# Four transposes between the products of the tile before, and an add ahead of a copy, in a matmul with bias and residual

## The chip, the cores and the metric

The kernel runs on one core of one Trainium2 chip. The metric is the device time of one execution in microseconds (us); it is given as the median of several runs. A profile is one more execution, recorded instruction by instruction; its span runs from the first to the last recorded instruction and is a little shorter than the device time.

The engines are named as in the profile: PE is TensorE's matmul, PEld its weight load, DVE is VectorE, ACT is ScalarE, POOL is GpSimd, and SP is the engine that issues all the DMAs here.

## What is computed

```python
batch, m, k, n = 16, 512, 1024, 768      # all float32
def reference(x, weight, bias, residual):
    return (np.matmul(x, weight) + bias + residual).astype(np.float32)
```

So 8192 rows of 1024 values are multiplied by one 1024 x 768 matrix, and a bias row and a residual of the output's shape are added.

## The kernel before

The 8192 rows are 64 tiles of 128 rows. Four groups of 16 tiles (S = 0 to 3) share the layout of the loads: row p*16 + j of a group is partition p of tile j, so that one DMA can bring several tiles.

A tile passes through these steps:

1. Its x arrives in a slot of `X` (16 slots). `cast` (lines 234 to 244, through `copy`, line 226) turns the 128 x 1024 float32 values into bfloat16 in `XB` (4 buffers); in the loop ScalarE does this, two tiles ahead.
2. `transp` (lines 246 to 253) takes two neighbouring bfloat16 values as one 32-bit word. TensorE transposes the 128 x 512 words in four steps of 128 x 128 into a PSUM buffer `PT` (2 buffers; line 250). The words themselves are the weights of such a step, and a float32 identity streams through. Then VectorE copies the whole buffer, 128 x 1024 as bfloat16, to `XT` (4 buffers; line 226).
3. `mm_all` (273 to 276) runs eight products, for q in 0..3 and e in 0..1. Each (`mm`, 265 to 271) loads 128 x 128 weights from `XT` (line 268) and streams 768 columns of the weight matrix as two matmuls of 512 and 256 columns (line 257), all into one PSUM accumulator `PO` of 128 x 768 float32. There are three of these (`HEAD = 3`).
4. `finish` (300 to 308) is VectorE's final add of a tile. For tiles below 14 it adds the bias to `PO` and puts the sum into a spare row; GpSimd adds the residual later. From tile 14 on, GpSimd has already added bias and residual in place (`pool_adds`, 286 to 298), and VectorE adds `PO` to that; it therefore waits for GpSimd.
5. The finished rows are stored from `R` by SP, in groups of up to 16 tiles.

The first tiles run in an order written out by hand (`HEAD_ORDER`), because there weights are still arriving; products of tiles 0 to 2 are interleaved, and the transposes of tiles 0 to 3 are done there. Tile 0's `finish` stands in that list too. The loop then takes tiles 3 to 62, and in each turn t the instructions are recorded in this order:

```python
    for t in range(HEAD, n_t):
        cast(t + 2)
        pool_adds(t + 1)
        transp(t + 1)
        if t < n_t - 1:
            mm_all(t, range(n_q))
        finish(t - 1)
        pool_adds(t + 1)
```

The last tile's products run column block by column block behind the loop (512 columns, then 256), so that the first block can be added and stored under the second.

`Program` keeps this recorded order on each engine: every engine runs its own instructions strictly in it. Between engines it derives waits from what an instruction reads and writes: a product's first weight load waits for VectorE's copy into `XT`, a first transpose for ScalarE's cast into `XB`, a copy for the fourth transpose, a first product into `PO` for the `finish` of the tile three before.

SP has one list of DMAs (`ORDER`), which goes on only when the first entry's needs have been recorded. On the chip SP also waits, at each DMA, for the work whose buffer it overwrites or stores.

Of the kernel before, what the change touches and what calls it, by code (L numbers as in the profile page):

```python
# [8 lines left out]
FP32 = mybir.dt.float32  # L9
BF16 = mybir.dt.bfloat16  # L10
P = 128
# [4 lines left out]
HEAD = 3  # L16
XT_N = 4
XB_N = 4
WARM = 12
EARLY_END = 14  # L20
TMP_ROW = 16
W_ROW = 14
# [95 lines left out]
def kernel(  # L118
# [14 lines left out]
    n_q = K // (2 * P)  # L133
    n_t = M // P
    chunks = [(0, 512), (512, N - 512)]
# [9 lines left out]
    def fixed(pool, name, n, shape, dt):  # L145
        return [pool.tile(shape, dt, name=f"{name}", tag=f"{name}{i}", bufs=1) for i in range(n)]
# [3 lines left out]
    XB = fixed(sb, "xb", XB_N, [P, K], BF16)  # L150
    XT = fixed(sb, "xt", XT_N, [P, n_q, P, 2], BF16)
    PO = fixed(ps, "psum_o", HEAD, [P, N], FP32)
    PT = fixed(ps, "pt", 2, [P, n_q, P], FP32)
# [8 lines left out]
    op = prog.add  # L162

    def rows(a, b, cs=range(len(chunks))):
        return [("R", r % RR, c) for r in range(a, b) for c in cs]
# [8 lines left out]
    def pump():  # L174
        while queue:
# [7 lines left out]
            elif kind == "r":  # L183
# [4 lines left out]
                if S < RR // J:  # L188
                    need += [("add", t) for t in range(EARLY_END) if TMP_ROW + t in at]
            else:  # L190
# [30 lines left out]
    def mark(*what):  # L221
        done.add(what)
        pump()

    def copy(eng, dst, src, rd, wr):
        op(eng, lambda e: (e.copy if eng == "act" else e.tensor_copy)(out=dst, in_=src), rd, wr)  # L226

    def plus(eng, dst, a, b, rd, wr):
        op(eng, lambda e: e.tensor_add(out=dst, in0=a, in1=b), rd, wr)  # L229
# [4 lines left out]
    def cast(t, how="s"):  # L234
        if t < n_t:
            assert ("x", t) in done, t
            src, dst, h = X[:, t % XR, :], XB[t % XB_N], K // 2
            rd, wr = [("X", t % XR)], [("XB", t % XB_N, i) for i in range(2)]
            if how == "sv":
                copy("act", dst[:, 0:h], src[:, 0:h], rd, wr[:1])  # L240
                copy("dve", dst[:, h:K], src[:, h:K], rd, wr[1:])
            else:
                copy("act" if how == "s" else "dve", dst, src, rd, wr)
            mark("cast", t)

    def transp(t):
        if t < n_t:
            words, pt = XB[t % XB_N].bitcast(FP32), PT[t % 2]
            for q in range(n_q):
                op("pe", lambda e, q=q: e.transpose(out=pt[:, q, :], in_=words[:, ts(q, P)], identity=ident),  # L250
                   [("XB", t % XB_N, 2 * q // n_q), "ident"], [("PT", t % 2)])
            copy("dve", XT[t % XT_N].rearrange("p q m e -> p (q m e)"),
                 pt.rearrange("p q m -> p (q m)").bitcast(BF16), [("PT", t % 2)], [("XT", t % XT_N)])

    def times(po, lhsT, rhs, first, final, rd, wr):
        def emit(e):
            return e.add_instruction(mybir.InstMatmult(  # L257
                name=nc.get_next_instruction_name(),
                ins=[e.lower_ap(rhs), e.lower_ap(lhsT, for_matmul_weights=True)], outs=[e.lower_ap(po)],
                start_tensor_calc=first, stop_tensor_calc=final,  # L260
                tile_size=(P, P), tile_position=(0, 0), ldweights=False,
            ))
        op("pe", emit, rd, wr)

    def mm(t, q, e, parts, po, wr):

        lhsT, rd = XT[t % XT_N][:, q, :, e], [("XT", t % XT_N)]
        op("pe", lambda g: g.ldweights(lhsT), rd)  # L268
        for n0, nl, to in parts:
            times(po[:, to:to + nl], lhsT, w_sb[:, q, e, n0:n0 + nl], q == 0 and e == 0, q == n_q - 1 and e == 1,  # L270
                  [*rd, ("w", q, e)], [wr])

    def mm_all(t, qs):
        for q in qs:
            for e in range(2):
                mm(t, q, e, [(n0, nl, n0) for n0, nl in chunks], PO[t % HEAD], ("PO", t % HEAD))

    def row(t, n0=0, nl=N):
        return R[:, t % RR, n0:n0 + nl]

    def tmp(t):
        return R[:, TMP_ROW + t, :]
# [3 lines left out]
    def pool_adds(upto):  # L286
        for t in [t for t in adds if t <= upto]:
            if ("r", t) not in done or (t < EARLY_END and ("fin", t) not in done):
                return
            adds.remove(t)  # L290
            r, rk = row(t), rows(t, t + 1)
            if t < EARLY_END:
                plus("pool", r, r, tmp(t), rk + rows(TMP_ROW + t, TMP_ROW + t + 1), rk)
                mark("add", t)
                mark("out", t)
            else:
                plus("pool", r, r, bias_sb, rk + ["bias"], rk)
                mark("add", t)

    def finish(t):  # L300
        p, pk = PO[t % HEAD], ("PO", t % HEAD)
        if t < EARLY_END:
            plus("dve", tmp(t), p, bias_sb, [pk, "bias"], rows(TMP_ROW + t, TMP_ROW + t + 1))
            mark("fin", t)
        else:
            assert ("add", t) in done, t
            plus("dve", row(t), p, row(t), [pk] + rows(t, t + 1), rows(t, t + 1))
            mark("out", t)

    def dummies(n, i):  # L310
        for _ in range(n):
            op("pe", lambda e: e.matmul(PO[i][:, 0:512], lhsT=warm[:, 0:P], rhs=warm, start=True, stop=True),  # L312
               ["warm"], [("PO", i)])
# [7 lines left out]
        out=ident, in_=ident, compare_op=mybir.AluOpType.not_equal, fill=1.0, base=0,  # L321
        pattern=[[-1, P]], channel_multiplier=1,
    ), ["ident"], ["ident"])
    dummies(WARM, 0)

    pump()
    for kind, *a in HEAD_ORDER:
        if kind == "bias":
            op("dve", lambda e: e.stream_shuffle(out=bias_sb, in_=bias_row, mask=[0] * QUAD), ["bias_row"], ["bias"])  # L329
        elif kind == "cast":  # L330
            cast(*a)
        elif kind == "fin":
            finish(a[0])
        elif kind == "warm":
            dummies(a[0], HEAD - 1)
        elif kind == "tr":
            transp(a[0])
        elif kind == "wc":
            q, e, eng = a
            r = W_ROW + 2 * q + e  # L340
            copy({"v": "dve", "s": "act", "g": "pool"}[eng], w_sb[:, q, e, :], w_st[:, 2 * q + e, :], rows(r, r + 1), [("w", q, e)])
            if (q, e) == (n_q - 1, 1):
                mark("wcast", q)
        else:
            mm_all(a[0], [a[1]])
    pump()
    for t in range(HEAD - 1):
        if ("fin", t) not in done:
            finish(t)
        pool_adds(t)  # L350

    for t in range(HEAD, n_t):
        cast(t + 2)
        pool_adds(t + 1)
        transp(t + 1)
        if t < n_t - 1:
            mm_all(t, range(n_q))
        finish(t - 1)
        pool_adds(t + 1)
    t = n_t - 1  # L360
    for i, (n0, nl) in enumerate(LAST):
# [46 lines left out]
```

## Time and profile before

| what | value |
|---|---|
| device time, median of 3 runs | 210.47 us (210.31 to 210.57) |
| span of the profiled execution | 208.5 us |
| PE busy | 201.6 us |
| VectorE, ScalarE, GpSimd busy | 105.3, 66.1, 115.2 us |
| mean granted TensorE clock | 0.996 |
| bytes moved | 87.20 MB, mean 418 GB/s |
| one product matmul of 512 columns, of 256 columns (mean length) | 379 ns, 273 ns |
| one transpose (mean length) | 274 ns |
| a copy `PT` to `XT` on VectorE | 691 ns |
| a final add on VectorE | 949 ns |
| a residual sum on GpSimd | 1817 ns |

The device time is taken outside the profile, and the span lies about 2 us below it. Matmuls are pipelined: the length of one includes its way through the array, and the next starts earlier, so a stream's pace is read from the distance of starts and not from the lengths. A line in the timeline merges neighbouring instructions of one kind; its second number is the time from the first start to the last end. In square brackets is the engine's idle time just before, and what ended it.

### The profile page before, as it was taken

What the parts mean: (1) busy time and instruction counts of PE and PEld (TensorE: products, weight loads), DVE (VectorE), ACT (ScalarE), POOL (GpSimd) and SP (SyncE); (2) the same over time, 40 slices, a digit from 0 to 9 for tenths busy, and PEclk for the clock granted to TensorE, in tenths of its full rate; (3) what the DMA queues carried; (4) which work ended last, traced back from release to release, by engine and by line L of the source; (5) the groups of instructions that cost most, each with busy time, mean ns of one, the idle gap of its engine ahead of it and who ended that gap; (6) DMA issues with size and microseconds to landing.
All of it is one profiled execution on the core that took longest, in us unless ns stands there. A gap on an engine that the chain in (4) does not pass through costs nothing.

```text
span 208.5 us, 2492 instructions
## 1 busy us (share of the span) xinstructions
PE 201.6 (97%) x1298; PEld 80.8 (39%) x794; DVE 105.3 (51%) x141; ACT 66.1 (32%) x69; POOL 115.2 (55%) x71
## 2 busy tenths in 40 slices
PE   7899999999999999999999999999999999999991
PEld 2333434443443444344334434433443443344340
DVE  1457555445545543654554454555445545544542
ACT  2444522402640282420280094230092047430000
POOL 1100029859999904999029801999207960899200
PEclk9999999999999999999999999999999999999998
DMA  5999999899999999999998999999999999999985
GB/s 216 425 425 445 426 423 475 385 427 425 485 409 416 449 395 438 453 396 437 410 493 387 432 445 429 443 443 385 423 450 468 416 398 471 415 443 417 427 351 232
DMA packets 4627, 87.20 MB, mean 418 GB/s; under 512 B 516, under 2 KB 644, under 8 KB 1416
## 3 DMA queue, kind: packets, MB, share of 16 engines
q1 hardware_dynamic: 4616, 87.05, 97.9%
q8 instruction: 8, 0.13, 0.2%
q14 instruction: 3, 0.02, 0.0%
HBM read 61.88 MB, written 25.17 MB: 417 GB/s over the span
## 4 chain that ended last, share of the span: by engine, by line
PE 92%; DMA 4%; DVE 1%; SPq 0%; ACT 0%; issue 0%
PE psum_o L257 79%; PE pt L250 13%; DMA x_tile<-in_x_dram 4%; SPq L168 0%; DVE xt L226 0%; ACT xb L226 0%; DVE ro L229 0%; SPq L403 0%; SPq L371 0%
## 5 line engine op out<-in xcount | busy, mean ns | idle before, releaser
L257 PE MATMUL psum_o<-w_sb,xt 128*128 128x256 bf16 (+1 forms) x1024 | 176.6, 326 | 0.5 <-DVE xt L226 0.5
L229 POOL TENSOR_TENSOR ro<-ro,bias_sb 128x768 f32<-128x768 f32 x50 | 88.8, 1817 | 46.9 <-DMA ro<-in_residual_dram 46.9
L226 ACT CAST xb<-x_tile 128x1024 bf16<-128x1024 f32 (+1 forms) x63 | 61.3, 1023 | 117.1 <-DMA x_tile<-in_x_dram 88.6
L268 PEld LDWEIGHTS <-xt 128*128 128x128 bf16 x520 | 50.9, 98 | 102.9 <-issue 101.0
L226 DVE COPY xt<-pt 128x1024 bf16<-128x1024 bf16 x64 | 44.1, 691 | 83.4 <-PE pt L250 83.4
L229 DVE TENSOR_TENSOR ro<-psum_o,ro 128x768 f32<-128x768 f32 (+2 forms) x51 | 47.6, 934 | 6.5 <-POOL ro L229 4.5
L250 PE MATMUL pt<-ident,xb 128*128 128x128 f32 x256 | 38.3, 274 | 0.6 <-DVE xb L226 0.4
L229 POOL TENSOR_TENSOR ro<-ro 128x768 f32<-128x768 f32 x14 | 24.9, 1818 | 25.0 <-DMA ro<-in_residual_dram 24.9
L250 PEld LDWEIGHTS pt<-ident,xb 128*128 128x128 f32 x256 | 29.7, 141 | 15.6 <-issue 12.3
L229 DVE TENSOR_TENSOR ro<-psum_o,bias_sb 128x768 f32<-128x768 f32 x14 | 13.2, 948 | 0.0
L312 PE MATMUL psum_o<-warm 128*128 128x512 bf16 x18 | 6.3, 506 | 1.4 <-DVE warm_a L232 1.4
L226 DVE CAST xb<-x_tile 128x512 bf16<-128x512 f32 (+1 forms) x4 | 1.9, 492 | 6.2 <-DMA x_tile<-in_x_dram 6.2
L226 ACT CAST w_sb<-ro 128x768 bf16<-128x768 f32 x4 | 3.3, 832 | 3.7 <-DMA ro<-in_weight_dram 3.7
L226 POOL CAST w_sb<-ro 128x768 bf16<-128x768 f32 x1 | 0.8, 822 | 6.0 <-DMA ro<-in_weight_dram 6.0
L312 PEld LDWEIGHTS psum_o<-warm 128*128 128x128 bf16 x18 | 2.1, 124 | 4.5 <-issue 2.7
L226 DVE CAST w_sb<-ro 128x768 bf16<-128x768 f32 x3 | 1.7, 557 | 2.0 <-DMA ro<-in_weight_dram 2.0
L226 ACT ACT_TABLE_LOAD x1 | 1.3, 1283 | 0.9 <-SPq L371 0.9
L329 DVE STREAM_SHUFFLE bias_sb<-bias_row 128x768 f32<-128x768 f32 x1 | 1.0, 1007 | 0.0
L232 DVE MEMSET warm<- 128x256 uint32 x1 | 0.3, 272 | 1.1 <-SPq L371 1.1
L232 DVE MEMSET bias_row<- 128x768 f32 x1 | 0.7, 698 | 0.2 <-issue 0.2
L232 POOL MEMSET ident<- 128x128 f32 x1 | 0.2, 204 | 0.5 <-SPq L371 0.5
L320 POOL TENSOR_SCALAR_AFFINE_SELECT ident<-ident 128x128 f32<-128x128 f32 x1 | 0.3, 292 | 0.2 <-POOL ident L232 0.2
(7 smaller groups left out, 0.7 us busy)
## 6 DMA issues: line engine op xcount, KB each, us to landing
out_dram<-ro SPq DMA_DIRECT2D x3, 6144.0 KB, 34.6
x_tile<-in_x_dram SPq DMA_DIRECT2D x3, 5120.0 KB, 24.5
ro<-in_residual_dram SPq DMA_DIRECT2D x3, 3840.0 KB, 32.4
x_tile<-in_x_dram SPq DMA_DIRECT2D x3, 3072.0 KB, 34.0
ro<-in_residual_dram SPq DMA_DIRECT2D x3, 2304.0 KB, 18.7
x_tile<-in_x_dram SPq DMA_DIRECT2D x4, 1024.0 KB, 10.9
x_tile<-in_x_dram SPq DMA_DIRECT2D x2, 2048.0 KB, 23.4
out_dram<-ro SPq DMA_DIRECT2D x1, 3840.0 KB, 13.3
```

Of the source, the lines that this page charges most:

```text
L226: op(eng, lambda e: (e.copy if eng == "act" else e.tensor_copy)(out=dst, in_=src), rd, wr)
L229: op(eng, lambda e: e.tensor_add(out=dst, in0=a, in1=b), rd, wr)
L232: op(eng, lambda e: e.memset(dst, v), [], [wr])
L250: op("pe", lambda e, q=q: e.transpose(out=pt[:, q, :], in_=words[:, ts(q, P)], identity=ident), [("XB", t % XB_N, 2 * q // n_q), "ident"], ...
L257: return e.add_instruction(mybir.InstMatmult(name=nc.get_next_instruction_name(), ins=[e.lower_ap(rhs), e.lower_ap(lhsT, for_matmul_weight ...
L268: op("pe", lambda g: g.ldweights(lhsT), rd)
L312: op("pe", lambda e: e.matmul(PO[i][:, 0:512], lhsT=warm[:, 0:P], rhs=warm, start=True, stop=True), ["warm"], [("PO", i)])
L320: op("pool", lambda e: e.affine_select(out=ident, in_=ident, compare_op=mybir.AluOpType.not_equal, fill=1.0, base=0, pattern=[[-1, P]], ch ...
L329: op("dve", lambda e: e.stream_shuffle(out=bias_sb, in_=bias_row, mask=[0] * QUAD), ["bias_row"], ["bias"])
```

## The change

In the loop, `transp(t + 1)` no longer stands ahead of the products of tile t. A new function `woven` runs the eight products of tile t and puts the four transposes of tile t + 1 one by one behind the second, third, fourth and fifth of them. The copy of the four transposes is recorded right behind the fourth, and `finish(t - 1)`, which stood behind it on VectorE, now stands ahead of it. In the last turn (t = 63) only `finish(62)` is left. `HEAD_ORDER` still uses `transp`, now made of the same two parts.

```diff
@@ -17,6 +17,7 @@
 XT_N = 4
 XB_N = 4
 WARM = 12
+WEAVE = 1
 EARLY_END = 14
 TMP_ROW = 16
 W_ROW = 14
@@ -243,14 +244,20 @@
                 copy("act" if how == "s" else "dve", dst, src, rd, wr)
             mark("cast", t)
 
+    def turn(t, q):
+        words, pt = XB[t % XB_N].bitcast(FP32), PT[t % 2]
+        op("pe", lambda e: e.transpose(out=pt[:, q, :], in_=words[:, ts(q, P)], identity=ident),
+           [("XB", t % XB_N, 2 * q // n_q), "ident"], [("PT", t % 2)])
+
+    def turned(t):
+        copy("dve", XT[t % XT_N].rearrange("p q m e -> p (q m e)"),
+             PT[t % 2].rearrange("p q m -> p (q m)").bitcast(BF16), [("PT", t % 2)], [("XT", t % XT_N)])
+
     def transp(t):
         if t < n_t:
-            words, pt = XB[t % XB_N].bitcast(FP32), PT[t % 2]
             for q in range(n_q):
-                op("pe", lambda e, q=q: e.transpose(out=pt[:, q, :], in_=words[:, ts(q, P)], identity=ident),
-                   [("XB", t % XB_N, 2 * q // n_q), "ident"], [("PT", t % 2)])
-            copy("dve", XT[t % XT_N].rearrange("p q m e -> p (q m e)"),
-                 pt.rearrange("p q m -> p (q m)").bitcast(BF16), [("PT", t % 2)], [("XT", t % XT_N)])
+                turn(t, q)
+            turned(t)
 
     def times(po, lhsT, rhs, first, final, rd, wr):
         def emit(e):
@@ -349,13 +356,23 @@
             finish(t)
         pool_adds(t)
 
+    def woven(t):
+
+        for q in range(n_q):
+            for e in range(2):
+                mm(t, q, e, [(n0, nl, n0) for n0, nl in chunks], PO[t % HEAD], ("PO", t % HEAD))
+                i = 2 * q + e - WEAVE
+                if t + 1 < n_t and 0 <= i < n_q:
+                    turn(t + 1, i)
+                    if i == n_q - 1:
+                        turned(t + 1)
+
     for t in range(HEAD, n_t):
         cast(t + 2)
         pool_adds(t + 1)
-        transp(t + 1)
+        finish(t - 1)
         if t < n_t - 1:
-            mm_all(t, range(n_q))
-        finish(t - 1)
+            woven(t)
         pool_adds(t + 1)
     t = n_t - 1
     for i, (n0, nl) in enumerate(LAST):
```

On the engines' queues this moves nothing but the transposes on TensorE and the adds on VectorE. The order on ScalarE, GpSimd and SP is as before. On VectorE an add gets a wait of its own for TensorE's last product; before, the copy ahead of it had already waited for a later TensorE instruction.

## The prediction

> **What bounds the kernel now.** I read the page first, then the waits, then the timeline of four places: one tile in the steady loop, the start of the loop, the first product that waits for a copy, and a tile whose residual comes late.
>
> The page says that TensorE is the bound: busy 97% of the span, at full clock, and the chain that ended last is almost all matmuls. The DMA queue is nearly as full, which matters below.
>
> ```profile
> span 208.5 us, 2492 instructions
> PE 201.6 (97%) x1298; PEld 80.8 (39%) x794; DVE 105.3 (51%) x141; ACT 66.1 (32%) x69; POOL 115.2 (55%) x71
> ...
> q1 hardware_dynamic: 4616, 87.05, 97.9%
> ...
> PE psum_o L257 79%; PE pt L250 13%; DMA x_tile<-in_x_dram 4%; SPq L168 0%; DVE xt L226 0%; ACT xb L226 0%; DVE ro L229 0%; SPq L403 0%; SPq L371 0%
> ```
>
> One tile of the steady loop, in the timeline (start, length, engine, line, what; x is how many were merged):
>
> ```profile
> 101.06 0.47 PEld L250 LDWEIGHTS pt<-ident,xb 128*128 128x128 f32 x4 [0.23 <-issue]
> 101.17 0.60 PE L250 MATMUL pt<-ident,xb 128*128 128x128 f32 x4
> 101.49 0.10 PEld L268 LDWEIGHTS <-xt 128*128 128x128 bf16 x1
> 101.60 2.76 PE L257 MATMUL psum_o<-w_sb,xt 128*128 128x512 bf16 x16
> 101.80 0.69 DVE L226 COPY xt<-pt 128x1024 bf16<-128x1024 bf16 x1 [1.48 <-PE pt L250]
> ...
> 102.41 0.95 DVE L229 TENSOR_TENSOR ro<-psum_o,ro 128x768 f32<-128x768 f32 x1
> ...
> 104.20 0.60 PE L250 MATMUL pt<-ident,xb 128*128 128x128 f32 x4
> ```
>
> The four transposes start at 101.17 and the products at 101.60, so a transpose costs 0.109 us of the stream; the tile period is 104.20 - 101.17 = 3.03 us, which leaves 2.60 for eight products, 0.325 each (216 ns for the 512-wide matmul and 109 for the 256-wide in the trace's nanosecond records). There is no idle time. Every weight load starts as the matmul ahead of it starts, and is hidden under it.
>
> **Part 1, the weave itself.** Per tile the same 8 pairs of matmuls and 4 transposes run. Before, the stream has one step from a product to a transpose (101.06 load, 101.17 transpose), three from transpose to transpose, one from transpose to product (101.49 load, 101.60 product); each is 0.109 us. Woven, it has four steps of the first kind and four of the third, each already seen. Could a transpose get cheaper because its float32 weights now hide under a product? After an idle engine its load is exposed:
>
> ```profile
> 6.51 0.33 PE L250 MATMUL pt<-ident,xb 128*128 128x128 f32 x1 [0.43 <-DVE xb L226]
> ```
>
> This one takes 0.33 instead of 0.27, so the load is worth 0.06, below the 0.109 that it hides under already; and the step from the last transpose to a product, whose bfloat16 load is shorter still, is also 0.109. So it is the transpose's own streaming that takes the time. Cost of part 1: 0. Its lower bound is 0.109 - 0.06 = 0.05 saved on each of 4 x 59 transposes, 11.6 us, if I misread what the 0.109 is; I keep it for a rival.
>
> **Part 2, the hand-off of a tile.** Before, the copy of the next tile's transposes has a whole tile to spare: 101.80 + 0.69 = 102.49, needed at 104.6. Woven, the fourth transpose stands behind the fifth product, so that only three products lie between it and the next tile's first weight load, which waits for the copy. What is available: 0.109 + 3 x 0.325 = 1.084 us from the start of that transpose. What is needed: 0.31 until the copy starts (101.493 to 101.803), 0.69 for the copy, then the signal to TensorE and the exposed part of the weight load. The last two show where a product waited for such a copy in the head:
>
> ```profile
> 11.47 1.29 DVE L226 COPY xt<-pt 128x1024 bf16<-128x1024 bf16 x2 [0.60 <-PE pt L250]
> ...
> 12.21 0.33 PEld L268 LDWEIGHTS <-xt 128*128 128x128 bf16 x2 [0.50 <-DVE xt L226]
> 12.22 0.50 PE L257 MATMUL psum_o<-w_sb,xt 128*128 128x512 bf16 x2 [0.26 <-DVE xt L226]
> ```
>
> The first of the two copies ends at 11.468 + 0.693 = 12.161, the load starts at 12.213 (0.052 later), the product at 12.217 and loses another 0.011 against a normal one: 0.015 behind the load. Sum: 0.310 + 0.692 + 0.052 + 0.015 = 1.069 of 1.084. It fits with 0.015 us to spare, so I take 0; the spread of the 59 steady copies' start is 0.309 to 0.311, which does not use it up. This is the tightest term. From the other side: if a load needed the whole 0.109 that it now has ahead of its matmul, the product would be late by 0.310 + 0.692 + 0.052 + 0.109 - 1.084 = 0.079; with the 0.06 of the transposes' load, by 0.03. I take 0 because the row at 12.21 is the very same load, and because a transposes' load that began 0.017 late (170.92 where the matmul ahead began at 170.90) left its matmul on time at 171.01.
>
> The Trainium skill, "TensorE: Matmul & The Clock Gate", section "LDWEIGHTS (loading the stationary operand)", speaks against this change: it gives a load as the number of columns over 1.2, 107 ns for 128. By it the product would be 0.077 us late in each of 59 tiles, some 4.5 us (an estimate from that page); the row at 12.21 shows 15 ns, and the measurement decides.
>
> **Part 3, the add ahead of the copy.** In the timeline above the add of tile t-1 (line 307, through 229) runs 0.81 us after the first product of tile t, behind the copy. Alone it could start when the last product of t-1 is done, about 0.20 after that point (a 256-wide product's end reaches VectorE 0.31 after its start), and end at 1.15; the fourth transpose starts at 5 x 0.325 + 3 x 0.109 = 1.95 and the copy is due at 1.95 + 0.31 = 2.26. So normally 1.1 us are free and the new place costs nothing. An explicit wait for TensorE is added to it, one queue instruction of about 0.07, inside that. But from tile 14 on the add also waits for GpSimd's sum of residual and bias, and now the copy, and so TensorE, stands behind it. The waits list shows VectorE held that way, and the worst case in the timeline:
>
> ```profile
> DVE ro L229 <- POOL ro L229: 4.5, 5, 1.7
> ```
>
> ```profile
> 80.34 2.76 PE L257 MATMUL psum_o<-w_sb,xt 128*128 128x512 bf16 x16
> ...
> 81.07 5.36 POOL L229 TENSOR_TENSOR ro<-ro,bias_sb 128x768 f32<-128x768 f32 x3 [8.46 <-DMA ro<-in_residual_dram]
> 82.92 0.96 DVE L229 TENSOR_TENSOR ro<-psum_o,ro 128x768 f32<-128x768 f32 x1 [1.68 <-POOL ro L229]
> ...
> 83.38 2.33 PE L257 MATMUL psum_o<-w_sb,xt 128*128 128x512 bf16 x13
> ...
> 83.79 0.68 DVE L226 COPY xt<-pt 128x1024 bf16<-128x1024 bf16 x1
> ```
>
> Here tile 23's products start at 80.34 and the residual of tile 22 has just landed (81.00; GpSimd's sum ends at 82.88). The add starts at 82.92. Before, only the add and a copy not yet needed were late. Woven, the copy for tile 24 comes behind that add: 82.915 + 0.873 (the distance at 83.79) = 83.788, its end 84.470, the product 0.067 later at 84.537. Due was 83.382: TensorE stands still for 1.155 us. The other late tiles, by the same sum: tile 17 (add at 63.80) would be about 0.26 late, 0.1 if GpSimd's chain comes 0.15 earlier thanks to earlier adds; tile 39 (add at 131.395) would have its next product at 133.02, due at 131.97, so 1.05. These are landing times, and they do not add up: once TensorE is 1.155 late, tile 39's residual is no longer late for it. That holds if landings stay where they are, and they should: the queue is full (97.9%), SP's order is unchanged, each long load is issued with over 6 us of earlier transfers still to run. Casts move up to 2 us later where they wait for transposes, and the loads behind them lie under the same backlog. Together: 1.155 (between 0, landings 1.2 us earlier, and 2.5, if every later landing moves with the delay).
>
> **Part 4, the start of the loop.** Tile 4's transposes, first in the loop, now fill a hole:
>
> ```profile
> 18.61 1.82 DVE L229 TENSOR_TENSOR ro<-psum_o,bias_sb 128x768 f32<-128x768 f32 x2
> 19.00 0.66 PE L250 MATMUL pt<-ident,xb 128*128 128x128 f32 x4
> 19.61 0.38 PE L257 MATMUL psum_o<-w_sb,xt 128*128 128x512 bf16 x1
> ```
>
> The first product of tile 3 waits until 19.61 for the first of the two adds (18.61 + 0.95, then 0.05), whatever the transposes do. Woven, these four come after 19.61 and cost 4 x 0.109 = 0.437 us on the stream; nothing gives it back at the other end, since the last tile's transposes stay inside tile 62.
>
> **Part 5, the end.** The last add, the last stores and their landing follow the last product; the DMA engines are 63% busy between 202.0 and 203.5, so the last stores start when issued and shift with TensorE.
>
> **Sum**: 0 + 0 + 1.155 + 0.437 = 1.59 us, on the span of 208.5, 210.1. The median of the runs is 210.47, 1.96 above the span for what lies around it; the same again gives 212.1.
>
> **The rivals.**
> - The hand-off is missed in every tile. For it: 0.015 us of slack on a sum of four terms, one seen in only one row. Against: that row is exact. It decides from 0.015 us more than I count. At 0.03 per tile it costs 59 x 0.03 = 1.8, of which 0.6 come before tile 24 and are part of the 1.155 there: 0.44 + 1.16 + 1.2 = 2.8, 213.2. At 0.079 it has swallowed the late residual: 0.44 + 4.66 = 5.1, 215.6.
> - The residual isn't late. If landings come 1.4% sooner (79.85 instead of 81.00), part 3 is free: 210.47 + 0.44 = 210.9. Against: loads are paced by a full queue. For: this is one execution.
> - Not slower: the transposes themselves get cheaper, a float32 load under a 0.325 us product rather than under the short transpose before it. It decides from 1.59 / 59 = 0.027 us per tile, 7 ns on each transpose. At its full 11.6 us the DMA queue becomes the bound: 0.979 x 208.5 = 204.1 us of transfers, 1.5 before and 1.6 behind them, 207.2 of span, 209.2. Against: the step from transpose to product above.
>
> **How the numbers follow.** Forecast 212.1 with chance 0.63, own range 211.4 to 212.7; hand-off missed 0.20; no late residual 0.11; cheaper transposes 0.06. The range 210.8 to 214.0 takes in the second rival and the lower half of the first, and leaves out about 0.14. A measurement tells 0.2%, 0.42 us, from no change: half of the "no late residual" case falls within it, and a corner of the cheaper transposes: same 0.07, faster 0.05, slower 0.88.
>
> **What would show it.** Right: a tile period of 3.04 as before; one idle stretch of TensorE of some 1.1 us near 83.4 released by the copy, with the add ahead of it released by GpSimd; products of tile 3 at 19.6 with no transposes before them. Wrong: idle time before most tiles' first load, released by the copy (first rival); transposes less than 0.109 apart from the product behind them (third); several late residuals that each stop TensorE.

## The result, and the profile after

| | before | after |
|---|---|---|
| device time, median (range) | 210.52 us (210.31 to 210.59) | 212.10 us (211.81 to 212.27) |
| ratio | | 1.0082, 95% interval 1.0068 to 1.0096 |
| span of the profiled execution | 208.5 us | 210.3 us |

The change makes the kernel 1.58 us slower; 212.1 had been forecast, and slower with 0.88. The page of the kernel after, its span, its engines and the chain that ended last:

```profile
span 210.3 us, 2515 instructions
PE 200.1 (95%) x1273; PEld 80.7 (38%) x794; DVE 110.4 (52%) x141; ACT 66.7 (32%) x69; POOL 115.2 (55%) x71
...
PE 57%; DMA 29%; POOL 10%; issue 1%; DVE 1%; SPq 0%; POOLq 0%
PE psum_o L264 49%; DMA ro<-in_residual_dram 26%; POOL ro L230 9%; PE pt L249 8%; DMA ro<-in_weight_dram 3%; DVE ro L230 0%; POOL w_sb L227 0%; DVE xt L227 0%; SPq L169 0%; SPq L420 0%; POOLq L105 0%; SPq L105 0%; SPq L388 0%
```

(25 product matmuls are missing from this record, 1273 instead of 1298, so PE's busy time reads a little low.) The chain is the news: before, 92% of it was TensorE. Now it goes from TensorE to GpSimd's residual sum and from there to the residual's transfer, which holds 26%.

First the steady tile, in the timeline of the kernel after:

```profile
100.57 0.27 PE L249 MATMUL pt<-ident,xb 128*128 128x128 f32 x1
...
101.00 0.27 PE L249 MATMUL pt<-ident,xb 128*128 128x128 f32 x1
...
101.44 0.27 PE L249 MATMUL pt<-ident,xb 128*128 128x128 f32 x1
...
101.87 0.27 PE L249 MATMUL pt<-ident,xb 128*128 128x128 f32 x1
...
102.18 0.69 DVE L227 COPY xt<-pt 128x1024 bf16<-128x1024 bf16 x1 [1.03 <-PE pt L249]
...
102.93 0.34 PEld L275 LDWEIGHTS <-xt 128*128 128x128 bf16 x2 [0.31 <-DVE xt L227]
103.16 0.96 DVE L230 TENSOR_TENSOR ro<-psum_o,ro 128x768 f32<-128x768 f32 x1 [0.28 <-PE psum_o L264]
...
103.61 0.27 PE L249 MATMUL pt<-ident,xb 128*128 128x128 f32 x1
```

Transposes now stand 0.434 us apart, which is one product (0.325) and one transpose (0.109). The first transposes of two tiles lie 103.61 - 100.57 = 3.04 us apart, the period of before. The hand-off of a tile is the way from its fourth transpose over VectorE's copy to its first product. The load at 102.93 waits for the copy (102.18 + 0.69 = 102.87, and 0.05), and its own idle time of 0.31 shows that; but in the trace's nanosecond records the product behind it starts 1.084 us after the fourth transpose, just when the stream is ready for it. In 58 of the 60 hand-offs that distance is 1.084 or 1.085.

In the other two an add stood ahead of the copy and waited for GpSimd's sum of residual and bias; below they are called the late residuals. Around the larger one, in the same timeline:

```profile
81.03 0.27 PE L249 MATMUL pt<-ident,xb 128*128 128x128 f32 x1
...
81.27 7.12 POOL L230 TENSOR_TENSOR ro<-ro,bias_sb 128x768 f32<-128x768 f32 x4 [8.94 <-DMA ro<-in_residual_dram]
...
82.34 0.27 PE L249 MATMUL pt<-ident,xb 128*128 128x128 f32 x1
82.44 1.14 PE L264 MATMUL psum_o<-w_sb,xt 128*128 128x512 bf16 x5
...
83.11 0.96 DVE L230 TENSOR_TENSOR ro<-psum_o,ro 128x768 f32<-128x768 f32 x1 [2.81 <-POOL ro L230]
83.99 0.68 DVE L227 COPY xt<-pt 128x1024 bf16<-128x1024 bf16 x1
84.73 0.83 PE L264 MATMUL psum_o<-w_sb,xt 128*128 128x512 bf16 x4 [1.14 <-DVE xt L227]
```

The transposes of tile 24 are complete at 82.6, and their copy could start at 82.65. It starts at 83.99, behind an add that waited for GpSimd, which waited for the transfer. The product comes 2.390 us after the fourth transpose instead of 1.084: 1.306 us lost. The same in small in turn 17: 1.256, 0.172 lost. There the add again waited for GpSimd, but no transfer had just landed: GpSimd's sum stood behind its own earlier ones, which ran without a break from 43.94 on.

```profile
61.65 3.58 POOL L230 TENSOR_TENSOR ro<-ro,bias_sb 128x768 f32<-128x768 f32 x2
...
63.57 0.96 DVE L230 TENSOR_TENSOR ro<-psum_o,ro 128x768 f32<-128x768 f32 x1 [1.68 <-POOL ro L230]
64.45 0.68 DVE L227 COPY xt<-pt 128x1024 bf16<-128x1024 bf16 x1
```

And the start of the loop:

```profile
18.46 2.68 DVE L230 TENSOR_TENSOR ro<-psum_o,bias_sb 128x768 f32<-128x768 f32 x3
19.47 0.81 PE L264 MATMUL psum_o<-w_sb,xt 128*128 128x512 bf16 x4 [0.67 <-DVE ro L230]
...
20.12 0.27 PE L249 MATMUL pt<-ident,xb 128*128 128x128 f32 x1
```

TensorE idles before 19.47, where the transposes of tile 4 stood; they follow behind the second product, at 20.12.

From the first product of tile 3 to the last matmul the kernel before takes 203.866 - 19.615 = 184.25 us, the kernel after 205.659 - 19.469 = 186.19. Of these 1.94 us, 1.306 + 0.172 are the late residuals, 0.437 the four transposes, and 0.02 is left.

### The profile page after: what moved, and what is told of

It is laid out like the page before. It is cut to its first block, busy times and chain, and to the rows that moved or that the text cites. A ratio compares the mean times of both kernels' runs of the same rounds, so it can differ in the third digit from the quotient of the medians.

```text
span 210.3 us, 2515 instructions
## 1 busy us (share of the span) xinstructions
PE 200.1 (95%) x1273; PEld 80.7 (38%) x794; DVE 110.4 (52%) x141; ACT 66.7 (32%) x69; POOL 115.2 (55%) x71
## 4 chain that ended last, share of the span: by engine, by line
PE 57%; DMA 29%; POOL 10%; issue 1%; DVE 1%; SPq 0%; POOLq 0%
PE psum_o L264 49%; DMA ro<-in_residual_dram 26%; POOL ro L230 9%; PE pt L249 8%; DMA ro<-in_weight_dram 3%; DVE ro L230 0%; POOL w_sb L227 0%; DVE xt L227 0%; SPq L169 0%; SPq L420 0%; POOLq L105 0%; SPq L105 0%; SPq L388 0%
## 5 line engine op out<-in xcount | busy, mean ns | idle before, releaser
L264 PE MATMUL psum_o<-w_sb,xt 128*128 128x256 bf16 (+1 forms) x999 | 190.9, 324 | 3.6 <-DVE xt L227 1.7
L249 PE MATMUL pt<-ident,xb 128*128 128x128 f32 x256 | 67.7, 273 | 0.8 <-DVE xb L227 0.6
L230 DVE TENSOR_TENSOR ro<-psum_o,ro 128x768 f32<-128x768 f32 (+2 forms) x51 | 48.1, 942 | 21.2 <-PE psum_o L264 14.8
L249 PEld LDWEIGHTS pt<-ident,xb 128*128 128x128 f32 x256 | 35.5, 141 | 56.4 <-issue 48.4
```

Of the source, the lines that this page charges most:

```text
L249: op("pe", lambda e: e.transpose(out=pt[:, q, :], in_=words[:, ts(q, P)], identity=ident), [("XB", t % XB_N, 2 * q // n_q), "ident"], [("P ...
L264: return e.add_instruction(mybir.InstMatmult(name=nc.get_next_instruction_name(), ins=[e.lower_ap(rhs), e.lower_ap(lhsT, for_matmul_weight ...
```

## The experiments

All were timed beside the kernel before on their own chip, which took 210.14 to 210.20 us there; differences are against that.

**The copy ahead of the add again, in every turn.** The transposes stay woven.

```diff
-        finish(t - 1)
         if t < n_t - 1:
             woven(t)
+        finish(t - 1)
```

> The weave is kept, but the final add of tile t-1 is recorded behind the copy again, in every turn. My theory (the weave itself is free; the start of the loop costs 0.44 us; the rest is the copy queued behind adds whose residual is late): no idle time of TensorE near 62 and 82 us, tile period 3.037 us throughout, 0.44 us slower than before: 210.96 us, and 1.1 us faster than the changed kernel. Rival (a little is lost in every one of 60 tiles, 1.58 / 60 = 0.026 us each): order of the add does not matter, 212.1 us.

Measured: 211.46 us, 1.0051 (1.0037 to 1.0065), 1.30 us above before. TensorE stops nowhere between 20 us and its end, as expected, and it ends 0.47 us later than before (last matmul at 204.34 against 203.87). But the expected 210.96 was 0.44 above a kernel before of 210.52, and here it is 1.30: 0.86 more. Neither theory gave this; something behind TensorE had become slower.

**Tile 4's transposes whole, the rest as changed.**

```diff
         pool_adds(t + 1)
+        if t == HEAD:
+            transp(t + 1)
         finish(t - 1)
...
-                if t + 1 < n_t and 0 <= i < n_q:
+                if t > HEAD and t + 1 < n_t and 0 <= i < n_q:
```

> As the changed kernel, but tile 4's four transposes and their copy stand whole ahead of tile 3's products, as before; from tile 4 on all is woven and the add comes first. My theory: the four run in the hole that ends at 19.6 us, 0.44 us are given back, the stop near 82 us stays and can grow, since TensorE comes there no later than in the changed kernel: 211.66 us. Rival (loss in every tile): one woven tile fewer, 212.1 us.

Measured: 211.75 us, 1.0071 (1.0055 to 1.0086), 1.59 above before: by the medians nothing was given back (the two intervals leave room for some 0.4). TensorE has 0.44 us less to do ahead of the late residuals and waits for them all the same: in its profile it loses 0.39 at tile 18, 0.89 at tile 24 and 0.10 at tile 40, 1.37 together, though tile 22's residual landed 0.48 earlier than in the changed kernel (80.713 against 81.196). What fixes the place is that landing: tile 24's first product starts 3.53 us behind it in the changed kernel, 3.52 here, and 3.52 in the kernel below with each transpose one product earlier. I had seen that the stop can grow and not drawn the conclusion: tile 24's product starts when the residual's transfer lets it, whatever stands before it. The two losses are not independent, and mending this one alone brought nothing that the medians show.

**Both.** Copy ahead of the add in every turn, and tile 4's transposes whole.

> Copy ahead of the add in every turn, and tile 4's transposes whole at the start of the loop; tiles 4 to 62 are woven. My theory: both losses gone, the same as before: 210.5 us within 0.15. Rival (0.026 us lost in each of 59 woven tiles): 212.1 us. A rival in which weaving gains but is hidden by the two losses: below 210.3 us.

Measured: 211.05 us, 1.0034 (1.0022 to 1.0046), 0.89 above. No expectation met. Yet the last matmul starts at 203.900, against 203.866 before, and from the first product of tile 3 it is 184.251 us in both: TensorE lost nothing. The 0.9 us lie behind it. The windows of 188 to 192 us show where (PE, PEld, DVE, ACT, POOL busy with counts, granted clock, DMA share, GB/s), first before:

```profile
188.00:192.00 4.00, 4.00 (x28) 1.51 (x15) 1.94 (x3) 0.00 (x0) 4.00 (x3) 1.00 0.99 427
```

```profile
188.41 16.55 SPq L168 DMA_DIRECT2D out_dram<-ro  x5
```

and this experiment, each with SP's timeline:

```profile
188.00:192.00 4.00, 3.95 (x28) 1.62 (x16) 2.03 (x3) 1.04 (x1) 4.00 (x4) 1.00 0.77 332
```

```profile
190.07 15.46 SPq L169 DMA_DIRECT2D out_dram<-ro  x5
```

The DMA engines are 77% busy there instead of 99%. How much that is worth depends on where the window is cut (from 187 to 194 us it is 92% instead of 95%); the landings show it without a window. The store of tiles 48 to 57 is issued at 190.07 and lands at 202.52; before it was issued at 188.41 and landed at 201.69. The last store lands at 208.02 instead of 207.27. The store of tiles 48 to 57 waits for the add of tile 57. With the woven copy ahead of it, an add starts 2.87 us after the next tile's first product; it was 0.81 in the kernel before and mostly 0.20 to 0.27 in the changed one. My reading: the store comes too late to follow the one ahead of it without a break, and the queue has no slack for it later. This was a reading of one profile, so it got its own test:

**Copy first up to turn 49, add first from turn 50 on**, tile 4's transposes whole.

```diff
-        finish(t - 1)
+        if t >= 50:
+            finish(t - 1)
         if t < n_t - 1:
             woven(t)
+        if t < 50:
+            finish(t - 1)
```

> As the kernel with copy first and tile 4's transposes whole, but from turn 50 on the add is recorded ahead of the copy, so that the last long stores start earlier. That kernel's products ended at 203.9 us as those of before do, yet it took 0.9 us longer; my theory now: its store of tiles 48 to 57 started 1.7 us later, the DMA engines ran dry near 190 us, and they set the end. Then this one has neither loss: 0 to 0.15 us below before. If instead the weave loses time in some way that the record of TensorE doesn't show, the 0.9 us stay.

Measured: 210.13 us, 0.9998 (0.9990 to 1.0007): as before. Windows of this run:

```profile
188.00:192.00 4.00, 4.00 (x29) 1.52 (x15) 1.99 (x3) 1.05 (x1) 4.00 (x3) 1.00 1.03 442
```

The DMA engines are full again, the store of tiles 48 to 57 lands at 201.39, and the 0.9 us are gone. (The edit moves the later stores too, so it shows that the late adds at the end cost the 0.9 us, and not which store alone.) TensorE again takes 184.251 us from the first product of tile 3 to the last matmul, as before. So 59 tiles of woven transposes cost nothing, and they gain nothing.

**The copy first in five turns alone**, those with a late residual in the profile before.

```diff
-        finish(t - 1)
+        if t not in (17, 23, 24, 39, 40):
+            finish(t - 1)
         if t < n_t - 1:
             woven(t)
+        if t in (17, 23, 24, 39, 40):
+            finish(t - 1)
```

> As the changed kernel, but in turns 17, 23, 24, 39 and 40 alone, where the residual came late in the profile before, the copy is recorded ahead of the add. My theory: those turns hold the whole of the second loss, so the time is that of the copy ahead of the add in every turn: 210.96 us. Rival (the add's place costs a little in every turn): 5/60 of the loss given back, 212.0 us.

Measured: 210.46 us, 1.0010 (1.0000 to 1.0019), 0.30 above before. Ahead of the copy, the add stops TensorE in these turns and nowhere else. TensorE ends 0.50 us later than before (204.367), the last store lands only 0.13 later (207.403 against 207.270): with the adds early, less is left in the DMA queue at the end. When the store of tiles 61 and 62 is issued, the one ahead of it has 1.34 us to go until it lands, against 1.81 before.

**The copy first in turns 17 and 23 alone.**

```diff
-        if t not in (17, 23, 24, 39, 40):
+        if t not in (17, 23):
```

and the same in the second condition.

> As the changed kernel, but in turns 17 and 23 alone, the two in which its profile shows TensorE stopped, the copy is recorded ahead of the add. If the delays do not add up, as I predicted, the residual that came late in turn 39 now stops TensorE itself: some 1.0 us there, 0.1 in turn 24, and the 0.44 of the start, with a little given back at the end: 1.2 to 1.5 us above before. If each late add costs on its own account, the two stops are simply gone, and the time is that of the kernel with five turns changed: 0.3 to 0.5 above before.

Measured: 211.58 us, 1.0068 (1.0056 to 1.0080), 1.44 above. Both stops seen in the changed kernel are taken away, and nearly the whole loss remains. VectorE in this run's timeline, then TensorE:

```profile
131.38 0.96 DVE L230 TENSOR_TENSOR ro<-psum_o,ro 128x768 f32<-128x768 f32 x1 [2.49 <-POOL ro L230]
132.26 0.68 DVE L227 COPY xt<-pt 128x1024 bf16<-128x1024 bf16 x1
```

```profile
131.04 1.14 PE L264 MATMUL psum_o<-w_sb,xt 128*128 128x512 bf16 x6
132.99 0.83 PE L264 MATMUL psum_o<-w_sb,xt 128*128 128x512 bf16 x4 [0.82 <-DVE xt L227]
```

Turn 39 stops TensorE now; the period there is 4.028 instead of 3.037 us, 0.99 lost. Tile 40's first product starts 3.59 us behind the landing of the residual it waited for, as in the two other kernels whose tile 40 is stopped (tile 4's transposes whole, and each transpose one product earlier). In the changed kernel it stopped nothing, because TensorE already ran behind. Late transfers set a time that TensorE can't pass; they do not add up. The stop in turn 24 did not come.

**Each transpose one product later** (`WEAVE = 2` instead of 1).

> As the changed kernel, but each transpose stands one product later, so that two products and not three lie behind the fourth one. It tests the sum of the hand-off, 1.07 us from the fourth transpose to the next product. My theory: 0.109 + 2 x 0.325 = 0.759 us are there, 0.31 us are missing in each of 60 tiles, 18.6 us; the late residuals vanish behind that; with the 0.44 of the start 229 us, period 3.35 us. If a weight load needed the 0.109 us that it normally has ahead of its product: 0.39 per tile, 234 us. If the signal were faster than the one row showed: less than 0.3 per tile, below 228.6.

Measured: 229.08 us, 1.0896 (1.0878 to 1.0914), with 229 expected. One hand-off in its timeline:

```profile
102.33 0.27 PE L249 MATMUL pt<-ident,xb 128*128 128x128 f32 x1
...
102.64 0.69 DVE L227 COPY xt<-pt 128x1024 bf16<-128x1024 bf16 x1 [1.67 <-PE pt L249]
...
103.38 0.33 PEld L275 LDWEIGHTS <-xt 128*128 128x128 bf16 x2 [0.63 <-DVE xt L227]
```

Now that the hand-off is exposed, it can be read off: 0.31 to the copy, 0.69 of copy, 0.05 to the load, and the tile's period is 3.347 us, 0.310 more. The needed 1.069 us are right to the hundredth, and so the 0.015 us to spare in the changed kernel are real. (The rival in the expectation, a load worth 0.109, comes to 0.40 per tile by its own terms and not 0.39; it stays as far off.)

**Each transpose one product earlier** (`WEAVE = 0`).

> As the changed kernel, but each transpose stands one product earlier, so that four products lie behind the fourth one and the hand-off has 0.34 us to spare instead of 0.015. My theory: the hand-off cost nothing before either, and the two late adds end when they did, so this is the changed kernel's time, 1.4 to 1.8 us above before. If the narrow hand-off cost time in every tile, this one gains it back: at most 0.7 us above before.

Measured: 211.81 us, 1.0078 (1.0063 to 1.0093), 1.61 above. With some twenty times the slack in every hand-off the time is that of the changed kernel. Its stops are 0.06, 1.03 and 0.43 us, in tiles 18, 24 and 40: again the late residuals.

**An attempt at a faster version**: the five turns, and tile 0's add ahead of tile 4's cast.

```diff
- ... ('bias',), ('cast', 4, 'sv'), ('mm', 0, 3),
- ('fin', 0), ('mm', 1, 3), ('mm', 2, 3)]
+ ... ('bias',), ('mm', 0, 3),
+ ('fin', 0), ('cast', 4, 'sv'), ('mm', 1, 3), ('mm', 2, 3)]
```

> The weave with the copy ahead of the add in the five late turns, and in addition tile 0's final add is recorded ahead of tile 4's cast, so that VectorE ends it near 18.7 us and not 19.6. Tile 3's products then start right behind those of tile 2, 0.8 us earlier, with tile 4's transposes woven into them. My theory: -0.81 + 0.44 = 0.37 us less on TensorE than before, of which the stores at the end pass on a half to all: 0.15 to 0.4 us below before. If the hole at 19 us is set by something else (tile 4's cast, weights), no gain: 0.3 above before as with the five turns alone.

Measured: 210.05 us, 0.9999 (0.9991 to 1.0008). TensorE in its timeline at the start of the loop:

```profile
17.36 2.55 PE L264 MATMUL psum_o<-w_sb,xt 128*128 128x256 bf16 x15
19.74 0.27 PE L249 MATMUL pt<-ident,xb 128*128 128x128 f32 x1
```

The hole is gone: tile 3's products run on from tile 2's. From the last product of tile 2 to the last matmul it is 203.779 - 18.980 = 184.80 us, against 203.866 - 18.688 = 185.18 before: 0.38 less, as worked out. The device time doesn't show it: the interval leaves room for 0.19 us of gain, no more. The head of this one execution ran 0.29 us later than that of before, but the edit didn't do that: the first product of tile 0 already starts 0.29 later (8.791 against 8.497), ahead of all that it moves. Why the rest isn't seen in the time stays open.

**That add's move alone, in the kernel before.** The same edit of the list, no weave.

> The kernel before with that one move alone: tile 0's final add ahead of tile 4's cast, no weave. The transposes of tile 4, ahead of tile 3's products, still wait for the cast, which ends near 19.0: the products start at 19.5 instead of 19.6, 0.1 us below before. So what the former run gains beyond that is the weave's.

Measured: 210.07 us, 0.9998 (0.9990 to 1.0007). The expected 0.1 us is within the noise, and so is the difference between this and the former run; they don't separate the weave's share.

## Why the prediction was right

*Part 1, the weave at no cost*: shown. The period stays at 3.037 us, each transpose takes 0.109, and the kernel that weaves 59 tiles and has neither loss takes the time of before, on TensorE's stream to the nanosecond (184.251 us). The third rival, transposes that get cheaper, fell with the same rows.

*Part 2, the hand-off with 0.015 us to spare*: shown from both sides, by the transposes one product later (0.310 us lost per tile, as the sum says) and earlier (nothing gained). The first rival fell. The Trainium skill ("TensorE: Matmul & The Clock Gate", section "LDWEIGHTS (loading the stationary operand)") gives a load as the number of columns over 1.2, 107 ns for 128. With that in place of the 0.015 us, the kernel with the later transposes would lose 0.402 us in each of 60 tiles and take some 235 us (an estimate from that figure); it took 229.08. A small slip in the prediction's reading: 57 of the 59 copies start 0.309 to 0.312 after their transpose, and the two others later, behind a late add; nothing rests on it.

*Part 3, the late residual*: right in place and mechanism, a little low in size. The forecast was 1.155 us; 1.306 + 0.172 = 1.478 were lost in the profiled execution. The 0.172 of turn 17, which the prediction put at 0.1 to 0.26 and left out of its sum, only moves a part of the delay ahead, since tile 24's place is fixed by the landing. The working holds: the residual landed at 81.196 instead of 81.005, and TensorE ran 0.146 ahead after an earlier start, and 1.155 + 0.191 + 0.146 = 1.49. So the term moves with the execution, by as much as the landing does. That delays do not add up was shown by the kernel with two turns mended, and by the fixed distance from landing to product. The second rival, no late residual, would have needed a landing 1.2 us earlier; in the profiles of all the runs it lies between 80.57 and 81.31.

*Part 4, 0.437 us at the start*: the size is right and was seen alone in the kernel with five turns mended: from the first product of tile 3 to the last matmul it takes 184.687 us, 0.436 more than before. What failed is the idea that it stands by itself: "nothing gives it back at the other end". Where late residuals set the pace, taking these 0.437 away brought nothing that the medians show.

*Part 5*: "the last stores start when issued and shift with TensorE" fits in its number and not in its mechanism. In the changed kernel the last matmul starts 1.793 us later and the last store lands 1.808 later. But two things cancel in that. The add of tile 62 and the store of tiles 61 and 62, first before, then after:

```profile
201.65 0.96 DVE L229 TENSOR_TENSOR ro<-psum_o,ro 128x768 f32<-128x768 f32 x1 [1.11 <-PE psum_o L257]
202.63 0.33 SPq L168 DMA_DIRECT2D out_dram<-ro  x1
```

```profile
203.82 0.96 DVE L230 TENSOR_TENSOR ro<-psum_o,ro 128x768 f32<-128x768 f32 x1 [0.74 <-PE psum_o L264]
204.81 0.33 SPq L169 DMA_DIRECT2D out_dram<-ro  x1
```

This store lands 3.65 us after its issue before (at 206.28, behind a store that lands 1.81 after that issue), and 3.27 after it in the changed kernel (208.07) and with five turns mended. So some 0.38 us are given back, and with five turns mended that is what one sees (0.50 on TensorE, 0.13 at the end). In the changed kernel the same store is issued only 0.85 us ahead of the last matmul instead of 1.24, because its add starts late, and that takes them away again. With the adds behind the copies, on the other hand, 0.9 us are lost though TensorE loses none. The step that failed is the one from engines 63% busy to stores that land a fixed time after their issue: the DMA queue is a second bound at the end.

*The sum*: 1.59 us were forecast on the span, and 1.81 came. That 212.1 was met all the same is luck. The prediction added 1.96 us, the median of the runs less the span of one profile. The changed kernel's profiled execution took 212.10 with a span of 210.32, 1.78 more, and in every execution on record for which both are listed the difference is 1.73 to 1.86. So the profile of before shows an execution of some 210.3 us (an estimate: 208.51 + 1.78) and not one of 210.47, and a term 0.18 too large made up for 0.21 that were missing.

*The chances*: slower got 0.88, and it was.

## What to carry to other kernels

Weaving short instructions between long ones was free here because each hidden step stayed hidden, and it gained nothing because nothing had been exposed: compare the distance of starts at each kind of step, transpose to transpose and transpose to product, before moving any. On an in-order engine, ask of the instruction that moves to the front what it can wait for that the one behind it can't: an add that waits for a transfer must not stand ahead of a copy that the bounding engine needs next. And an add that no engine waits for may still feed a store: here, where DMA is as full as TensorE, adds 2 us later cost 0.9 us at the end. Before a profile's span is turned into a device time, ask whether that profile was a typical execution.

## What the runs showed that I had not expected

- The final add of tile 62 started 0.45 us after its wait for TensorE was over in the changed kernel (203.37 to 203.82), 0.07 in the kernel before. It was 0.43 with tile 4's transposes whole and the add first, and with the transposes one product earlier, and 0.07 in the kernels with two or five turns mended. GpSimd's sum for that tile had ended long before (192.46). The cause stays open.
- A fixed signal time: from the end of VectorE's copy to the waiting weight load it is 52 to 55 ns in every exposed hand-off of these runs, and from the start of a transpose to the copy that waits for nothing else 308 to 312.
